# Forming the adaLN modulations of a four-layer network on TensorE alone, 256 columns at a time

## The chip, the cores and the metric

The program runs on one core of a Trainium2 chip, in one launch. The metric is device time in microseconds (us), as the median of three runs; one further execution was profiled, and all rows below are from that one.

## What is computed

Four layers (one mLSTM and differential attention layer, one convolution and mixture-of-experts layer, two hybrid attention layers) work on 256 tokens of width 1024, in fp32. Each is modulated by vectors that depend only on a condition vector c:

```python
def adaln(cond, w, b):
    return jax.nn.silu(cond) @ w + b

# layers 0 and 1: w is 1024 x 6144, six vectors of 1024 each
sh_m, sc_m, gt_m, sh_f, sc_f, gt_f = jnp.split(adaln(c, mod_w, mod_b)[:, None, :], 6, axis=-1)
sh_c, sc_c = jnp.split(adaln(c_ctx, mod_w, mod_b), 6, axis=-1)[:2]      # layer 0 only
# layers 2 and 3: w_ada is 1024 x 3072
shift, scale, gate = jnp.split(c @ w_ada + b_ada, 3, axis=-1)
u = x * (1.0 + scale[:, None, :]) + shift[:, None, :]
```

So each modulation is a product of one row (for the first two vectors of layer 0, of two rows) with a weight matrix: 72 MB of weights in all, read once, with hardly any arithmetic. Everything else of the program (projections, attention, FFN, experts) is products of 256 or 512 tokens with weights.

## The kernel before

All weights come through one stream. `Model.plan` lists them in the order of use; `Stream` loads each as two halves of 512 KB into a ring of eight `raw` buffers of 128 x 1024 (line 164, on SP's DMA queue), and for a projection weight splits each half into an exact high part `hi` (ScalarE, line 98) and a remainder `lo` (VectorE, line 99). The projections then run as three matmuls in a fast fp32 form each (`mm3`, lines 92 to 94: hi x hi, lo x hi, hi x lo). A ring buffer comes free when its last reader is done, and only then is the next load issued.

The modulation weights are items of the same plan, woven between the projection weights (`weave`): 8 items for the first modulation stand alone at the start, about four after each projection weight of layer 0, some 2.75 after each of the four output weights, and the last 24 among the 33 weights of layer 0's FFN. An item is 128 rows of the matrix by 2048 columns, 1 MB, and eight of them make one piece (there are ten pieces; in the last piece of layer 2 and of layer 3 an item has 1024 columns and 0.5 MB). `Ada` treats it in one of two ways.

- The first piece (`vec` is false) multiplies on TensorE: the stationary operand is the condition for these 128 rows, 32 columns wide, and the output lands in one of four groups of 32 PSUM partitions, which are four column groups of TensorE (line 357, `adap<-raw,cond`).
- The other nine pieces (`vec`) scale and add rows elsewhere, in `sum_rows`: the left half of the item on VectorE (lines 337 and 340, tile `adac`), the right half is scaled on ScalarE (lines 338 and 341) and added on GpSimd in two pieces of 512 columns (line 343). After the eighth item TensorE sums the 128 partitions by ones (line 357, `adap<-adac,ones`).

After the eighth item of a piece ScalarE copies the sums out of PSUM (line 364), TensorE transposes them (line 367), and VectorE adds the bias (line 370).

The order of instructions on each engine is made when the program is built, by a list scheduler; each engine then works strictly in that order. So an instruction that waits holds up all that stands behind it on its engine. The PSUM bank that the modulations use (`bg`, one buffer) is shared with the rows that `bcast_row` spreads (line 384).

The names that the rows use: `pf` and `pk` are outputs of layer 0's projections, `rp` rope, `mscan` a running maximum over 256 tokens in 16 dependent steps (line 600), `ds`/`de` and `X`/`E`/`kq`/`pn` the two kinds of attention, `po` the output projection, `ph`/`py` the two products of an FFN, `diag` constants for the convolution that GpSimd prepares (line 1014).

Of the kernel before, what the change touches and what calls it, by code (L numbers as in the profile page):

```python
# [12 lines left out]
F32 = mybir.dt.float32  # L13
# [3 lines left out]
AF = mybir.ActivationFunctionType  # L17
# [14 lines left out]
class Env:  # L32


    def __init__(self, nc, tc, ctx, raw_bufs, split_bufs):
        self.nc, self.tc, self.ctx = nc, tc, ctx
        self.raw_bufs = raw_bufs
        self.cst = ctx.enter_context(tc.tile_pool(name="cst", bufs=1))
        self.small = ctx.enter_context(tc.tile_pool(name="small", bufs=4))
        self.rawp = ctx.enter_context(tc.tile_pool(name="rawp", bufs=raw_bufs))  # L40
        self.splp = ctx.enter_context(tc.tile_pool(name="splp", bufs=split_bufs))
        self.bgp = ctx.enter_context(tc.tile_pool(name="bgp", bufs=2))
        self.bgc = ctx.enter_context(ExitStack())
        self.bgps = self.bgc.enter_context(tc.tile_pool(name="bgps", bufs=1, space=PSUM))
        self.adac = ExitStack()
        self.adasb = self.adac.enter_context(tc.tile_pool(name="adasb", bufs=1, side="right"))
        self.consts()

    def consts(self):
        nc, cst = self.nc, self.cst  # L50
        self.ident = cst.tile([128, 128], F32, name="ident")
        make_identity(nc, self.ident)
        self.identb = cst.tile([128, 128], BF, name="identb")
        nc.vector.tensor_copy(self.identb, self.ident)
        self.ones = cst.tile([128, 128], F32, name="ones")
        nc.vector.memset(self.ones, 1.0)
        zeros = self.adasb.tile([128, 128], F32, name="zeros")
        nc.vector.memset(zeros, 0.0)
        self.mhalf = cst.tile([128, 16], F32, name="mhalf")
        nc.vector.memset(self.mhalf, -0.5)  # L60

        self.tri_le = cst.tile([128, 128], F32, name="tri_le")
        nc.gpsimd.affine_select(self.tri_le, self.ones, [[1, 128]], OP.is_ge, 0.0, base=0, channel_multiplier=-1)
        self.tri_ge = cst.tile([128, 128], F32, name="tri_ge")
        nc.gpsimd.affine_select(self.tri_ge, self.ones, [[-1, 128]], OP.is_ge, 0.0, base=0, channel_multiplier=1)
        self.neg_le = cst.tile([128, 128], BF, name="neg_le")
        nc.gpsimd.affine_select(self.neg_le, zeros, [[1, 128]], OP.is_ge, NEG, base=0, channel_multiplier=-1)
        self.neg_ge = cst.tile([128, 128], BF, name="neg_ge")
        nc.gpsimd.affine_select(self.neg_ge, zeros, [[-1, 128]], OP.is_ge, NEG, base=0, channel_multiplier=1)
# [210 lines left out]
def layout(inputs):  # L280

    a = {k: np.ascontiguousarray(v) for k, v in inputs.items()}
    b = np.zeros((2, 2, 32), np.float32)
    b[:, :, :8] = a.pop("l0_mlstm_gate_b").reshape(2, 2, 8).transpose(1, 0, 2)
    a["gate_b"] = b.reshape(128)
    for g, names in GROUPS.items():
        a[g] = np.ascontiguousarray(np.concatenate([a.pop(k).reshape(-1, 128) for k, _ in names]).T)
    a["lambdas"] = np.concatenate([a.pop("l0_lambda_" + k) for k in ("q1", "q2", "k1", "k2")])
    a["cmp_w1_2"] = np.ascontiguousarray(a["cmp_w1_2"].reshape(2, 2, 16, 128, 64).transpose(0, 1, 3, 2, 4)).reshape(2, 2, 128, 1024)
    a["cmp_w2_2"] = np.concatenate([a["cmp_w2_2"]] * 2, 3)  # L290
    w = a["l0_w_in"]
    a["l0_w_in"], a["l0_w_gate"] = blocks256(w, ORDER), blocked(w, (MG, 32))
    for k in ("l0_ffn_w1", "l0_ffn_w3", "l1_conv_pw1_w", "l1_moe_w1", "l1_moe_w3"):
        a[k] = blocks256(a[k])
    w = a["w_in_2"]
    a["w_in_2"] = np.concatenate([blocked(w, *c) for c in CH], -1)
    a["rope0"] = np.concatenate(rope_axial(), 1)
    a["rope2"] = np.concatenate(rope_plain(64) + rope_plain(32), 1)
    return a
# [12 lines left out]
class Ada:  # L312
# [2 lines left out]

    def __init__(self, e, w, c0, n=2048, vec=False):
        self.e, self.n, self.vec = e, n, vec
        self.items = []  # L320
        for k in range(KB):
            h = [[(w[128 * k:128 * k + 128, c0 + n // 2 * j:c0 + n // 2 * (j + 1)].rearrange("(a p) f -> p a f", p=128),
                   0, n // 2)] for j in range(2)]
            self.items.append(((1, n // 2, h), lambda *t, k=k: self.step(k, t)))

    def bind(self, cond, bias, *out, plus1=None):
        self.cond, self.bias, self.out, self.plus1 = cond, bias, out, plus1

    def sum_rows(self, k, halves):

        e, nc = self.e, self.e.nc
        if k == 0:
            self.acc = e.adasb.tile([128, 2, 1024], F32, tag="adac", name="adac")
        a, (x, y) = self.acc[:, :, :self.n // 2], (h[:, 0, :] for h in halves)
        c = self.cond[:, k, 0:1]
        if k == 0:
            nc.vector.tensor_scalar(a[:, 0], x, c, None, op0=OP.mult)
            nc.scalar.activation(a[:, 1], y, AF.Copy, scale=c)
        else:
            nc.vector.scalar_tensor_tensor(a[:, 0], x, c, a[:, 0], op0=OP.mult, op1=OP.add)  # L340
            nc.scalar.activation(y, y, AF.Copy, scale=c)  # L341
            for i in range(0, self.n // 2, 512):
                nc.gpsimd.tensor_tensor(a[:, 1, i:i + 512], a[:, 1, i:i + 512], y[:, i:i + 512], op=OP.add)  # L343

    def step(self, k, halves):
        e, nc, n = self.e, self.e.nc, self.n
        vec, last = self.vec, k == KB - 1
        if vec:
            self.sum_rows(k, halves)
        if vec and not last:  # L350
            return
        if vec or k == 0:
            self.p = e.bgps.tile([128, 512], F32, tag="bg", name="adap")
        q4 = n // 4
        for j in range(4):
            h = self.acc[:, j // 2] if vec else halves[j // 2][:, 0, :]
            nc.tensor.matmul(self.p[32 * j:32 * j + 32, :q4], e.ones[:, 0:32] if vec else self.cond[:, k, :],
                             h[:, q4 * (j % 2):q4 * (j % 2) + q4],
                             start=(vec or k == 0), stop=last, skip_group_check=True)
        if not last:  # L360
            return
        nb = n // 512
        r = e.bgp.tile([128, 512], F32, tag="adar", name="adar", bufs=1)
        e.ada_read = nc.scalar.copy(r[:, :q4], self.p[:, :q4])
        q = e.bgps.tile([128, 512], F32, tag="bg", name="bg")
        for b in range(nb):
            nc.tensor.transpose(q[:, 128 * b:128 * b + 128], r[:, 128 * b:128 * b + 128], e.ident)
        v = q[:, :128 * nb].rearrange("p (b j r) -> p j b r", b=nb, j=4)
        for i, o in enumerate(self.out):
            nc.vector.tensor_tensor(o.rearrange("p (j b) -> p j b", j=4), v[:, :, :, i],  # L370
                                    self.bias.rearrange("p (j b) -> p j b", j=4), op=OP.add)
            if self.plus1 is not None:
                a, b = self.plus1
                nc.vector.tensor_scalar(o[:, a:b], o[:, a:b], 1.0, None, op0=OP.add)


def bcast_row(e, col, out, n=8):
# [1516 lines left out]
class Model:  # L1894
    def __init__(self, e, I, x, O):
        self.e, self.I, self.x, self.O = e, I, x, O
        self.ada = {}
        if "l0_mod_w" in I:
            for i in range(3):
                self.ada[0, i] = Ada(e, I["l0_mod_w"], 2048 * i, vec=i > 0)  # L1900
        if "l1_mod_w" in I:
            for i in range(3):
                self.ada[1, i] = Ada(e, I["l1_mod_w"], 2048 * i, vec=True)
        if "w_ada_2" in I:
            for l in range(2):
                for i in range(2):
                    self.ada[2 + l, i] = Ada(e, I["w_ada_2"][l], 2048 * i, 2048 - 1024 * i, vec=True)

    def items(self, *keys):
        return [i for k in keys if k in self.ada for i in self.ada[k].items]  # L1910
# [28 lines left out]
    def vecs(self):  # L1939
# [18 lines left out]
        for l in range(2):  # L1958
# [3 lines left out]
            if l == 0:  # L1962
                yield
                with e.tc.issue_after(e.ada_read.ins) if hasattr(e, "ada_read") else ExitStack():
                    load_cols(e, V, I, "vc", q=nc.scalar)
        cond = V["c_2"][:, :, None]
        for l in range(2):
            if (2 + l, 0) in self.ada:
                b = V["b_ada_2"][:, 24 * l:24 * l + 24]
                mods(2 + l, 0, cond, b[:, 0:16], plus1=(8, 16))  # L1970
                mods(2 + l, 1, cond, b[:, 16:24], 8, plus1=(0, 8))
        yield

    def gain(self, mod, g, name):
# [327 lines left out]
```

## Time and profile before

| | us |
|---|---|
| median of three runs | 2024.3 (2023.06 to 2024.95) |
| the profiled execution | 2031.13 |
| its span, first to last instruction | 2029.4 |
| TensorE busy in the span | 1873.0 (92%) |
| VectorE busy | 1582.0 (78%) |
| ScalarE busy | 1189.8 (59%) |
| GpSimd busy | 517.9 (26%) |

The profiled execution is 6.8 us over the median; its span leaves 1.7 us of it outside. Busy shares are averages over stages with different limits, so the stages are to be read apart: from 28 to 392 us layer 0's projections, attention and output projection run, from 392 to 580 us its FFN, then the convolution (to 780), the experts (to about 1550) and the two hybrid layers. The modulations are formed from 0 to 580 us. A matmul that is shown as busy includes the time in which it drains while the next one already runs, so TensorE's busy time overstates its work.

### The profile page before, as it was taken

The numbers are of one execution on the slowest core, as the hardware profiler recorded it, in microseconds if no ns is written. First come the engines' busy times: TensorE is split into PE (matmuls) and PEld (weight loads), VectorE is DVE, ScalarE is ACT, GpSimd is POOL, SyncE is SP. The second block draws the span as 40 slices with busy tenths as digits, with TensorE's granted clock in tenths as the row PEclk, the third lists the DMA queues.
The fourth block names the chain that finished last, engine by engine and source line by source line (L and its number), as shares of the span: only waits on it lengthen the run. The fifth ranks groups of instructions, "written<-read, shape, count | busy, mean of one in ns | idle before, by whom it ended". The sixth has DMA issues, their size and how long they took to land. (4 is left out here: it accounts for less than half of the span.)

```text
span 2029.4 us, 33102 instructions
## 1 busy us (share of the span) xinstructions
PE 1873.0 (92%) x12339; PEld 1657.9 (82%) x12339; DVE 1582.0 (78%) x2239; ACT 1189.8 (59%) x1838; POOL 517.9 (26%) x460
## 2 busy tenths in 40 slices
PE   6789889699997779999999999999997899989997
PEld 3768667699976668999999999999996888878886
DVE  5887996677669758999999999999996674568455
ACT  5455564455545447777777777777776443454333
POOL 2645662533227531000000000000001523333141
PEclk8889987799998889999999999999998988988889
DMA  9845775288753128999999999999993431233120
GB/s 361 285 154 208 244 242 178 80 323 308 250 208 127 50 83 322 366 342 338 346 365 351 333 354 358 342 342 355 355 355 115 135 105 63 89 130 111 65 72 21
DMA packets 132462, 468.41 MB, mean 231 GB/s; under 512 B 14994, under 2 KB 16274, under 8 KB 132292
## 3 DMA queue, kind: packets, MB, share of 16 engines
q1 hardware_dynamic: 131008, 464.38, 64.2%
q8 instruction: 99, 1.62, 0.3%
q10 hardware_dynamic: 1172, 1.65, 0.2%
q14 instruction: 71, 0.58, 0.1%
q0 software_dynamic: 112, 0.17, 0.1%
HBM read 465.10 MB, written 1.05 MB: 230 GB/s over the span
## 5 line engine op out<-in xcount | busy, mean ns | idle before, releaser
L99 DVE TENSOR_TENSOR lo<-raw,hi 128x1024 fp32r<-128x1024 f32 x678 | 858.1, 1280 | 134.9 <-ACT hi L98 112.3
L98 ACT CAST hi<-raw 128x1024 fp32r<-128x1024 f32 x718 | 747.1, 1050 | 300.4 <-PE ph L94 92.8
L93 PE MATMUL ph<-lo,gh 128*128 128x256 f32 x1408 | 397.0, 282 | 3.6 <-DVE lo L99 1.8
L94 PE MATMUL ph<-hi,gl 128*128 128x256 f32 x1408 | 396.7, 282 | 0.0
L92 PE MATMUL ph<-hi,gh 128*128 128x256 f32 x1408 | 394.0, 280 | 0.0
L93 PEld LDWEIGHTS ph<-lo,gh 128*128 128x128 f32 x1408 | 264.6, 188 | 12.6 <-DVE lo L99 6.9
L94 PEld LDWEIGHTS ph<-hi,gl 128*128 128x128 f32 x1408 | 264.8, 188 | 3.4
L92 PEld LDWEIGHTS ph<-hi,gh 128*128 128x128 f32 x1408 | 264.8, 188 | 2.8
L343 POOL TENSOR_TENSOR adac<-adac,raw 128x512 f32<-128x512 f32 x112 | 194.0, 1757 | 180.1 <-ACT raw L341 109.0
L1597 POOL MEMSET kv<- 64x2 f32 x4 | 0.4, 97 | 791.8 <-DVE lo L99 775.1
L99 POOL TENSOR_TENSOR lo<-raw,hi 128x1024 fp32r<-128x1024 f32 (+1 forms) x40 | 97.5, 2446 | 186.9 <-ACT hi L98 178.5
L93 PE MATMUL pe<-lo,hhi 128*128 128x512 f32 x352 | 138.0, 393 | 0.0
L92 PE MATMUL pe<-hi,hhi 128*128 128x512 f32 x352 | 137.2, 397 | 0.5 <-ACT hhi L98 0.5
L94 PE MATMUL pe<-hi,hlo 128*128 128x512 f32 x352 | 125.8, 392 | 0.0
L92 PE MATMUL ht<-hi,Hh 128*128 128x256 f32 (+1 forms) x384 | 117.8, 307 | 0.6 <-ACT u L459 0.6
L93 PE MATMUL ht<-lo,Hh 128*128 128x256 f32 (+1 forms) x384 | 116.0, 302 | 0.0
L94 PE MATMUL ht<-hi,Hl 128*128 128x256 f32 (+1 forms) x384 | 115.8, 302 | 0.0
L92 PE MATMUL ph<-Fh,hi 128*128 128x256 f32 x352 | 101.5, 290 | 11.4 <-DVE h L980 8.8
L93 PE MATMUL ph<-Fl,hi 128*128 128x256 f32 x352 | 101.4, 289 | 0.0
L94 PE MATMUL ph<-Fh,lo 128*128 128x256 f32 x352 | 100.2, 287 | 0.0
L92 PEld LDWEIGHTS ht<-hi,Hh 128*128 128x128 f32 x384 | 79.6, 207 | 2.3 <-ACT u L459 1.4
L1083 POOL TENSOR_TENSOR cyp<-cyp,ctp 128x256 f32<-128x256 f32 x83 | 72.4, 883 | 34.8 <-ACT ctp L1082 31.2
(592 smaller groups left out, 4124.3 us busy)
## 6 DMA issues: line engine op xcount, KB each, us to landing
raw<-in_l_moe_w SPq DMA_DIRECT2D x528, 512.0 KB, 5.3
raw<-in_l_mod_w SPq DMA_DIRECT2D x96, 512.0 KB, 5.4
raw<-in_l_ffn_w SPq DMA_DIRECT2D x66, 512.0 KB, 4.9
raw<-in_w_in SPq DMA_DIRECT2D x60, 512.0 KB, 3.5
raw<-in_w_ada SPq DMA_DIRECT2D x32, 512.0 KB, 5.4
raw<-in_l_w_in SPq DMA_DIRECT2D x28, 512.0 KB, 5.6
raw<-in_l_conv_pw_w SPq DMA_DIRECT2D x24, 512.0 KB, 4.3
raw<-in_w_ada SPq DMA_DIRECT2D x32, 256.0 KB, 3.7
```

What stands on the lines that cost most here:

```text
L92: mm(out, a[0], b[0], start=start, stop=False, **kw)
L93: mm(out, a[0], b[1], start=False, stop=False, **kw)
L94: return mm(out, a[1], b[0], start=False, stop=stop, **kw)
L98: nc.scalar.copy(hi, src)
L99: (lo_eng or nc.vector).tensor_tensor(lo, src, f32(hi), op=OP.subtract)
L343: nc.gpsimd.tensor_tensor(a[:, 1, i:i + 512], a[:, 1, i:i + 512], y[:, i:i + 512], op=OP.add)
L1083: nc.gpsimd.tensor_tensor(yp, yp, t, op=OP.add)
L1597: nc.gpsimd.memset(kv[64:128, :, T - 1:T], 0.0)
```

## The change

All items are now blocks of 256 columns by all 1024 rows (the host lays the three weight matrices out so, as it does for the FFN weights), and every one is multiplied on TensorE. An item takes eight matmuls of 256 columns: for each of the four column groups two, with different 128-row blocks of the weights (`L336` in the rows of the changed kernel). ScalarE copies the 128 x 256 result out (`L339`); TensorE sums the four groups and turns the row into columns with two matmuls whose moving operand `rows4` is one column wide (two for the first piece), `L342`; VectorE adds the bias (and one, where a scale is meant) in one instruction on two columns for each output (`L348`). `sum_rows` is gone. A piece of 2048 columns is still 8 items of 1 MB; one of 1024 columns is 4 items of 1 MB instead of 8 of 0.5 MB, so the items are 72 instead of 80, and 16 instead of 24 of them stand in the FFN.

```diff
+        self.rows4 = cst.tile([128, 3], F32, name="rows4")
+        nc.vector.tensor_reduce(self.rows4, self.ident.rearrange("p (j r) -> p r j", j=4)[:, 0:3, :], axis=AX.X, op=OP.add)
...
-    for k in ("l0_ffn_w1", "l0_ffn_w3", "l1_conv_pw1_w", "l1_moe_w1", "l1_moe_w3"):
+    for k in ("l0_ffn_w1", "l0_ffn_w3", "l1_conv_pw1_w", "l1_moe_w1", "l1_moe_w3", "l0_mod_w", "l1_mod_w", "w_ada_2"):
         a[k] = blocks256(a[k])
...
-    def sum_rows(self, k, halves):
...
-            nc.vector.scalar_tensor_tensor(a[:, 0], x, c, a[:, 0], op0=OP.mult, op1=OP.add)
-            nc.scalar.activation(y, y, AF.Copy, scale=c)
-            for i in range(0, self.n // 2, 512):
-                nc.gpsimd.tensor_tensor(a[:, 1, i:i + 512], a[:, 1, i:i + 512], y[:, i:i + 512], op=OP.add)
...
+    def __init__(self, e, w, c0, n=2048):
+        self.e, self.n = e, n
+        self.items = [(kchunk(w[c0 // 256 + i])[0], lambda *t, i=i: self.step(i, t)) for i in range(n // 256)]
...
+        p = e.bgps.tile([128, 512], F32, tag="bg", name="adap")
+        for f in range(2):
+            for j in range(4):
+                k = 2 * j + f
+                nc.tensor.matmul(p[32 * j:32 * j + 32, :256], self.cond[:, k, :], halves[k // 4][:, k % 4, :],
+                                 start=(f == 0), stop=(f == 1), skip_group_check=True)
+        r = e.bgp.tile([128, 256], F32, tag="adar", name="adar")
+        e.ada_read = nc.scalar.copy(r, p[:, :256])
+        m = len(self.out)
+        for b in range(2):
+            nc.tensor.matmul(p[:, 256 + m * b:256 + m * b + m], r[:, 128 * b:128 * b + 128], e.rows4[:, self.first:self.first + m],
+                             start=True, stop=True, skip_group_check=True)
...
+        for r, o in enumerate(self.out):
+            nc.vector.scalar_tensor_tensor(o[:, cs], v[:, :, r], float(one), self.bias[:, cs], op0=OP.add, op1=OP.add)
```

How the orders move, at three places. The first is TensorE while it makes the first projection (`pf`) and the transposes of the context (`xt`) just after the start. Before, no modulation stands there:

```order
L92 MATMUL pf<-Uh,hi 128x256
L93 MATMUL pf<-Ul,hi 128x256
L94 MATMUL pf<-Uh,lo 128x256
L426 MATMUL xt<-ident,raw 128x128 x16
L92 MATMUL pk<-hi,Uh 128x256
```

In the changed kernel the first woven item (`L336`) opens half-way through these 48 matmuls and stands between them and the transposes (this is the end of the piece; its line numbers are higher by 3 for `mm3`):

```order
L95 MATMUL pf<-Uh,hi 128x256
L96 MATMUL pf<-Ul,hi 128x256
L97 MATMUL pf<-Uh,lo 128x256
L336 MATMUL adap<-raw,cond_114 32x256 x7
L400 MATMUL xt<-ident,raw 128x128 x8
L342 MATMUL adap<-rows_87,adar 128x1 x2
L400 MATMUL xt<-ident,raw 128x128 x8
L336 MATMUL adap<-raw,cond_114 32x256 x8
L95 MATMUL pk<-hi,Uh 128x256
```

So the transposes, and all behind them, now wait for the loads of the first woven item.

The second place is VectorE in the running maximum `mscan` of the gates. Before, sums of the modulation rows (`L340`) and weight splits (`L99`) stand between its steps (`L600`):

```order
L600 TENSOR_TENSOR mscan_635<-mscan_636 32x256
L340 SCALAR_TENSOR_TENSOR adac<-raw,cond_112,adac 128x1024
L600 TENSOR_TENSOR mscan_635<-mscan_636 32x256
L673 TENSOR_TENSOR rp_738<-rp_738,rp_739 128x512
L600 TENSOR_TENSOR mscan_636<-mscan_635 32x256
L99 TENSOR_TENSOR lo<-raw,hi 128x1024
L340 SCALAR_TENSOR_TENSOR adac<-raw,cond_112,adac 128x1024
```

In the changed kernel the same steps (`L574`) follow each other, with one small bias addition between them:

```order
L647 TENSOR_TENSOR rp_819<-rp_819,rp_820 128x512
L574 TENSOR_TENSOR mscan_716<-mscan_715 32x256
L574 TENSOR_TENSOR mscan_715<-mscan_716 32x256
L348 SCALAR_TENSOR_TENSOR mod_1_169<-adap,vb 128x2
L574 TENSOR_TENSOR mscan_715<-mscan_716 32x256
L574 TENSOR_TENSOR mscan_716<-mscan_715 32x256 x2
```

The rows of 1024 columns have left VectorE's order here.

The third place is TensorE in the FFN, where `py` and `ph` follow each other. Before, TensorE meets a modulation there only where a piece ends, as here:

```order
L92 MATMUL ph<-Fh,hi 128x256
L357 MATMUL adap<-adac,ones 32x512
L93 MATMUL ph<-Fl,hi 128x256
L94 MATMUL ph<-Fh,lo 128x256
L92 MATMUL ph<-Fh,hi 128x256
```

In the changed kernel 16 items stand between the matmuls of the FFN, one after every 70 to 120 of them, and the two narrow matmuls (`L342 MATMUL adap<-rows_87,adar 128x1 x2`) of each some 23 rows behind it; only the last one stands behind the last `py`:

```order
L96 MATMUL py<-lo,hhi 128x512
L97 MATMUL py<-hi,hlo 128x512
L336 MATMUL adap<-raw,cond_114 32x256 x8
L95 MATMUL ph<-Fh,hi 128x256
L96 MATMUL ph<-Fl,hi 128x256
L97 MATMUL ph<-Fh,lo 128x256
```

The multiplications have moved into the middle of TensorE's run of FFN matmuls.

## Rows read from the trace of the kernel before

**Rows 1.** Windows: busy us (instructions) of PE, PEld, DVE, ACT, POOL; clock; DMA share; GB/s.

```profile
28.00:392.00 364.00, 305.37 (x1830) 255.25 (x1831) 299.70 (x407) 194.81 (x346) 202.79 (x189) 0.86 0.62 212
392.00:580.00 188.00, 186.51 (x1262) 167.66 (x1260) 121.89 (x136) 97.54 (x129) 47.75 (x31) 0.99 0.75 262
```

**Rows 2.** Waits of TensorE, 28 to 392 us: total us, times, longest.

```profile
PE pf L92 <- DVE rp L671: 10.1, 1, 10.1
PE ph L92 <- DVE h L980: 8.8, 1, 8.8
PE pt L453 <- DVE xs L938: 7.4, 1, 7.4
PE X L745 <- DVE mixd L847: 6.1, 1, 6.1
PE ds L839 <- DVE de L837: 5.8, 3, 4.6
PE ds L831 <- DVE mscan L610: 4.1, 1, 4.1
```

**Rows 3.** Waits of TensorE, 392 to 580 us; the longest of them.

```profile
PE bg L384 <- DVE mod L370: 0.7, 1, 0.7
```

**Rows 4.** Groups, 28 to 392 us: busy us, mean ns, idle before.

```profile
L343 POOL TENSOR_TENSOR adac<-adac,raw 128x512 f32<-128x512 f32 x84 | 147.7, 1788 | 61.5 <-ACT adac L338 23.5 <-ACT raw L341 23.2 <-issue 13.2
...
L340 DVE SCALAR_TENSOR_TENSOR adac<-raw,cond,adac 128x1024 f32<-128x1024 f32 x35 | 62.4, 1782 | 1.1 <-DMA raw<-in_l_mod_w 0.9
L98 ACT CAST hi<-raw 128x1024 fp32r<-128x1024 f32 x45 | 46.9, 1054 | 42.8 <-PE po L94 10.5 <-DMA raw<-in_l_ffn_w 10.3 <-PE pf L93 6.3
...
L340 DVE SCALAR_TENSOR_TENSOR adac<-raw,vc,adac 128x1024 f32<-128x1024 f32 x7 | 13.6, 1937 | 0.0
...
L357 PE MATMUL adap<-adac,ones 128*32 128x512 f32 x44 | 11.6, 605 | 1.2 <-DVE adac L340 1.2
```

**Rows 5.** Groups, 392 to 580 us.

```profile
L357 PE MATMUL adap<-adac,ones 128*32 128x256 f32 (+1 forms) x28 | 6.1, 482 | 0.0
```

**Rows 6.** Timeline of TensorE near 14 us: start us, us; a matmul gives two records.

```profile
13.88 1.06 PE L357 MATMUL adap<-raw,cond 128*32 128x512 f32 x8
```

**Rows 7.** Timeline, 84 to 120 us, the instructions of TensorE around one pair of sums.

```profile
86.36 0.27 PE L94 MATMUL pf<-Uh,lo 128*128 128x256 f32 x1
...
86.57 1.05 PE L357 MATMUL adap<-adac,ones 128*32 128x512 f32 x4
...
87.55 0.57 PE L566 MATMUL gkq<-ident,grow 104*128 104x104 f32 x4
```

**Rows 8.** Timeline, 572 to 580 us: the same sums with 256 columns, their copy, a bias addition.

```profile
576.80 0.63 PE L357 MATMUL adap<-adac,ones 128*32 128x256 f32 x4
...
577.55 0.36 ACT L364 COPY adar<-adap 128x256 f32<-128x256 f32 x1
...
578.93 0.16 DVE L370 TENSOR_TENSOR mod<-bg,vc 128x8 f32<-128x8 f32 x1
```

**Rows 9.** Line 2146, the router: 16 matmuls in fp32 with 8 moving columns; min/median/max ns.

```profile
L2146 PE MATMUL bg<-rw,ru x32: 175/256/361, 736.8 to 740.3; 128*128 128x8 f32 x32
```

**Rows 10.** Timeline of VectorE, 100 to 117 us: steps of the running maximum.

```profile
104.14 0.41 DVE L600 TENSOR_TENSOR mscan<-mscan 32x256 f32<-32x256 f32 x1
...
105.92 1.51 DVE L600 TENSOR_TENSOR mscan<-mscan 32x256 f32<-32x256 f32 x1
```

**Rows 11.** Timeline of VectorE and of GpSimd, 369 us on.

```profile
369.80 16.30 DVE L99 TENSOR_TENSOR lo<-raw,hi 128x1024 fp32r<-128x1024 f32 x3
...
373.07 3.26 POOL L1014 TENSOR_TENSOR diag<-ident,vd 128x128 f32<-128x128 f32 x9
```

**Rows 12.** SP's queue and TensorE's timeline near 40 us; a load's median us to landing.

```profile
38.66 9.95 SPq L164 DMA_DIRECT2D raw<-in_l_mod_w  x8
...
42.45 0.30 PE L426 MATMUL xt<-ident,raw 128*128 128x128 f32 x1 [1.70 <-ACT mghi L98]
...
raw<-in_l_mod_w SPq DMA_DIRECT2D x96, 512.0 KB, 5.4
```

More of the change, by code (lines that the diff above doesn't have):

```diff
@@ L312 @@
 class Ada:
[L318 to L327, printed above, removed]
@@ L329, in sum_rows @@
-    def sum_rows(self, k, halves):
-        e, nc = self.e, self.e.nc
[L332 to L339, printed above, removed]
-            nc.vector.scalar_tensor_tensor(a[:, 0], x, c, a[:, 0], op0=OP.mult, op1=OP.add)
-            nc.scalar.activation(y, y, AF.Copy, scale=c)
-            for i in range(0, self.n // 2, 512):
-                nc.gpsimd.tensor_tensor(a[:, 1, i:i + 512], a[:, 1, i:i + 512], y[:, i:i + 512], op=OP.add)
@@ L345, in step @@
[L345 to L374, printed above, removed]
@@ new lines, in __init__, with bind, step @@
+    def __init__(self, e, w, c0, n=2048):
+        self.e, self.n = e, n
+        self.items = [(kchunk(w[c0 // 256 + i])[0], lambda *t, i=i: self.step(i, t)) for i in range(n // 256)]
+    def bind(self, cond, bias, *out, plus1=None, first=0):
+        self.cond, self.bias, self.out, self.plus1, self.first = cond, bias, out, plus1, first
+    def step(self, i, halves):
+        e, nc = self.e, self.e.nc
+        p = e.bgps.tile([128, 512], F32, tag="bg", name="adap")
[10 more added lines that the diff above has]
+                             start=True, stop=True, skip_group_check=True)
+        v = p[:, 256:256 + 2 * m].rearrange("p (b r) -> p b r", r=m)
+        cs = slice(2 * i, 2 * i + 2)
+        one = self.plus1 is not None and self.plus1[0] <= 2 * i < self.plus1[1]
+        for r, o in enumerate(self.out):
+            nc.vector.scalar_tensor_tensor(o[:, cs], v[:, :, r], float(one), self.bias[:, cs], op0=OP.add, op1=OP.add)
@@ L1899, in __init__ @@
             for i in range(3):
-                self.ada[0, i] = Ada(e, I["l0_mod_w"], 2048 * i, vec=i > 0)
+                self.ada[0, i] = Ada(e, I["l0_mod_w"], 2048 * i)
         if "l1_mod_w" in I:
             for i in range(3):
-                self.ada[1, i] = Ada(e, I["l1_mod_w"], 2048 * i, vec=True)
+                self.ada[1, i] = Ada(e, I["l1_mod_w"], 2048 * i)
         if "w_ada_2" in I:
@@ L1906, in __init__ @@
                 for i in range(2):
-                    self.ada[2 + l, i] = Ada(e, I["w_ada_2"][l], 2048 * i, 2048 - 1024 * i, vec=True)
+                    self.ada[2 + l, i] = Ada(e, I["w_ada_2"][l], 2048 * i, 2048 - 1024 * i)
     def items(self, *keys):
@@ L1965, in vecs @@
                     load_cols(e, V, I, "vc", q=nc.scalar)
-        cond = V["c_2"][:, :, None]
+        if "c_2" in V:
+            nc.vector.tensor_copy(cond[:, :, 2], V["c_2"])
         for l in range(2):
@@ L1969, in vecs @@
                 b = V["b_ada_2"][:, 24 * l:24 * l + 24]
-                mods(2 + l, 0, cond, b[:, 0:16], plus1=(8, 16))
-                mods(2 + l, 1, cond, b[:, 16:24], 8, plus1=(0, 8))
+                mods(2 + l, 0, cond, b[:, 0:16], plus1=(8, 16), first=2)
+                mods(2 + l, 1, cond, b[:, 16:24], 8, plus1=(0, 8), first=2)
         yield
```

## Prediction, before the changed kernel ran

> **What bounds the kernel now.** I first asked for the windows of the two stages in which the modulations are formed [rows 1]. From 28 to 392 us (layer 0 without its FFN) TensorE and VectorE are both busy some 82 to 84% of 364 us, and the granted clock of TensorE averages 0.86, so part of the time it ran at 1.2 and not 2.4 GHz. From 392 to 580 us (the FFN) TensorE is busy 186.5 of 188 us at a clock of 0.99, VectorE 122. Then I read whom TensorE waits for. In the FFN its longest wait is 0.7 us [rows 3]: there TensorE's own matmuls set the end, and nothing that VectorE, ScalarE or GpSimd is relieved of can shorten it. Before it, six waits of four to ten us stand out, all for VectorE [rows 2]. The groups of that stage show what VectorE does meanwhile [rows 4]: 42 additions of modulation rows take 76 us of its 300, and GpSimd is busy 148 us with the other half of the same rows. GpSimd seems to slow VectorE as well: the same step of the running maximum takes 0.41 us in one place and 1.51 us in another, where VectorE and GpSimd both work on modulation rows [rows 10].
>
> So the change relieves one engine in a stage where it is one of two that bind, and loads the other, in that stage and in one that it binds alone. The stages after 580 us hold nothing of the change.
>
> **What an item costs TensorE.** Eight matmuls of 256 columns, two for each column group. The trace has the same kind: four of 512 columns, one in each group, take 1.06 us together [rows 6], no more than two take (1.05) [rows 7], so the groups run at once. With 256 columns it is 0.63 [rows 8]; 256 columns thus stream in 1.05 - 0.63 = 0.42 us, and an item in 0.85. What it displaces is longer, since the array changes between four groups and the whole: from the last full matmul before such a pair, at 86.36, to the next full instruction, at 87.55, is 1.19 us, of which the last matmul itself has about 0.12 (the following pair of rows would start that much later) [rows 7]. That is 1.07 for the streaming of 512 columns with both changes.
>
> On such changes the Trainium skill has a rule that speaks against the kernel: TensorEngine Tiling, Key Properties, says that changing the tiling mode drains TensorE. By [rows 7] a change costs about 0.1 us on either side, which is less than the drain that a group shows beyond its streaming (0.63 - 0.42 = 0.21 us); if each change waited for a full drain of that length, as the rule would have it, the 64 items would cost 64 x 2 x 0.11 = 14 us more than I count.
>
> The two narrow matmuls behind an item have 128 x 128 fp32 weights and one moving column. The nearest row is the router's, with such weights and 8 columns: 32 records from 736.8 to 740.3 us, 0.11 us each [rows 9]; a matmul is two records, so the two cost 0.45 us. The Trainium skill would make them cheaper: TensorEngine Tiling, Instruction Overhead, gives each matmul about 60 cycles and a single column the time of 60. At 2.4 GHz that is an estimate of 0.1 us for the four records, or 22 us less over 64 items; the row has the same weights, so I go by it.
>
> An item is therefore 1.07 + 0.45 = 1.52 us of TensorE at full clock. Below, without the changes and with half the records, 0.85 + 0.22 = 1.07; above, with both changes drained, 1.07 + 0.22 + 0.45 = 1.74. Over the 64 new items that is 97 us, between 68 and 111. The eight items of the first piece were on TensorE before; they pass while the first 8 MB load, and I count them at nothing (what shows of them, the last one's narrow matmuls, replaces four transposes).
>
> The other engines gain. ScalarE copies 128 x 256 in 0.36 us and VectorE adds a bias in 0.16 us an item [rows 8]; the 48 items before the FFN give VectorE 8 us for the 76 it loses.
>
> **The FFN.** 16 items at 1.52 are 24 us. The last stands behind the last matmul of the FFN, beside the residual: 23 us remain. Removed are 28 records of sums, 6 us [rows 5], and 12 transposes (four for each of three pieces), which at the 0.14 us of the transposes of `gkq`, four in 0.57 [rows 7], are 2. With TensorE the bound [rows 1, 3] the difference goes straight into the time: **+15 us**. No cover is left there that could hide it.
>
> **Before the FFN.** 48 items at 1.52 are 73 us. Removed are 44 records of sums, which as eleven groups of four at 1.07 make 12 us [rows 4, 7], and 24 transposes, 3 us. So TensorE gets 58 us more work in a stage of 364 us in which it is shown busy 305 [rows 1]. What is given back:
> - the waits for VectorE: rope 10.1, `mixd` 6.1, `de` 5.8 and `mscan` 4.1 us, 26 in all [rows 2]. They stand behind work that leaves VectorE. I take them all. The other two I leave: `h` (8.8) comes after three splits that took 16.3 us while GpSimd made the convolution's `diag` [rows 11], which stays, and `xs` (7.4) is the end of the residual's chain.
> - the clock. At 0.86 over 364 us, of which TensorE is busy 84%, at most 0.14 x 364 x 0.84 = 43 us are lost to the lower level. Items in the gaps make TensorE steadier; I take a third, 14. Nothing excludes 0 or all.
> - places where TensorE has nothing else: the order puts five items ahead of the output projection and two beside the residual, seven items, of which I take six as free, 9 us.
> Against it stand:
> - the start. The first woven item now stands ahead of the context's transposes. Its loads are issued from 38.66 us on [rows 12]; with 5.4 us to land, the first half is there at about 44, while the transposes began at 42.45. With the item's own 1 to 2 us and the second half behind it, 4 us. VectorE's free time may win it back by the next chunk.
> - new waits. Each item adds a step TensorE to ScalarE, back to TensorE, to VectorE, and only then is the one PSUM bank free. The scheduler has put some 23 matmuls between, near 2.8 us, for a copy of 0.36. I take 4 us in all; nothing bounds this from the trace but ScalarE's queue (below).
>
> Sum: 58 - 26 - 14 - 9 + 4 + 4 = **+17 us**.
>
> **Sum.** 17 + 15 = 32 us. On the profiled execution, 2031.1 us, that gives 2063; it is 7 us over the median of the runs, so on the median it gives **2056 us**, 1.6% slower. The price of an item moves it by -29 or +14.
>
> **The rivals.**
> - *VectorE alone bound the stage before the FFN.* Then its relief pays for TensorE's new work there, and only the FFN's 15 us show: 2039 us. For it speak [rows 2]; against it TensorE's 305 us, which with 58 more fill 363 of 364 unless the clock rises.
> - *It comes out faster.* The one mechanism is the clock: if the items keep TensorE at 2.4 GHz from 28 to 392 us, all 43 us come back and not 14, and the items cost the lower bound, 1.07. Then the 48 items cost 22 us less (0.45 each) and the work is 58 - 22 = 36; less 26, 43 and 9, plus 4 for the start, that makes -38. In the FFN 15 items at 1.07 less the 8 removed are +8. Together -30: 2024 - 30 = 1994 us. It decides in favour of the change once stage one ends 15 us earlier. Against it: part of the lower clock lies at the very start and around the residual, where TensorE waits for chains that no item fills.
> - *The coupling.* TensorE works in order, and so does ScalarE. If the narrow matmuls of an item find ScalarE in one cast (1.05 us, [rows 4]) that the scheduler did not foresee, TensorE stands for it: 64 x 1.05 = 67 us, of which perhaps half lie in the pass of the 23 matmuls ahead. 2056 + 36 = 2092 us. For it speaks that ScalarE is kept waiting itself before its casts, 43 us [rows 4]; against it the distance.
>
> **How the numbers follow.** My sum and its near surroundings (2043 to 2075) get 0.50, the first rival 0.17, the faster one 0.13, the coupling 0.20. The range leaves out the faster rival and the upper part of the coupling: 2024 to 2090. A measurement of this kernel can tell some 0.2% (4 us) from no change: faster 0.14, the same 0.06, slower 0.80.
>
> **What would show it.** In the changed profile: the FFN, from its first to its last `py`, longer by 15 us with no new waits; an item's eight matmuls with their narrow ones, 1.5 us apart from the rest; the waits for rope, `mixd`, `de` and `mscan` gone; VectorE some 70 us less busy before the FFN and GpSimd almost idle; the first `ph` about 17 us later. I am wrong if the FFN does not grow (then TensorE was not its bound, or the groups run faster than the rows say), or if the clock before the FFN comes near 1.0 and the first `ph` earlier, or if waits of TensorE for the copies (`adar`) or for loads add up to more than 10 us.

## The result, and the profile after

The changed kernel takes 2099.95 us (median of four runs, 2097.31 to 2100.62) where the kernel before, run beside it, takes 2024.62: a ratio of 1.0364 with the 95% interval [1.0343, 1.0386], or 75 us. The forecast was slower by 32 us, 2056 us, with a range to 2090. The profiled execution of the changed kernel has a span of 2095.6 us, 66 more than that of before (whose profiled execution was 6.8 us over its median, while this one is 2.6 under).

The program is cut by what TensorE starts: the first projection matmul (`pf`), the first `ph` and the first and last `py` of the FFN. The windows of the kernel before between these points are (columns as in [rows 1]):

```profile
31.10:365.80 334.70, 287.29 (x1718) 238.82 (x1718) 274.85 (x391) 182.16 (x329) 176.90 (x134) 0.87 0.64 219
405.20:576.90 171.70, 171.70 (x1164) 154.79 (x1164) 114.56 (x124) 89.74 (x116) 46.84 (x29) 1.00 0.80 279
```

and those of the changed kernel, with the stretch before the first `pf` ahead of them:

```profile
0.00:50.80 50.80, 28.45 (x176) 15.79 (x176) 14.78 (x45) 15.77 (x28) 4.71 (x18) 1.00 0.81 288
50.80:423.80 373.00, 343.77 (x2614) 271.05 (x2614) 162.23 (x382) 143.18 (x321) 30.29 (x54) 0.91 0.54 192
456.20:644.70 188.50, 188.50 (x1414) 165.41 (x1416) 85.60 (x107) 74.53 (x104) 0.57 (x1) 1.00 0.70 233
```

| stretch | before | after | difference | forecast |
|---|---|---|---|---|
| start to first `pf` | 31.1 | 50.8 | +19.7 | 0 (the 4 us for the start were laid to the transposes behind it) |
| first `pf` to first `ph` | 334.7 | 373.0 | +38.3 | +17 |
| first `ph` to first `py` | 39.4 | 32.4 | -7.0 | 0 |
| first to last `py` | 171.7 | 188.5 | +16.8 | +15 |

So the FFN came as forecast, and the two earlier stretches did not. VectorE did lose its rows before the FFN (275 to 162 us busy) and GpSimd almost everything (177 to 30). TensorE took 56 us more busy time there, and its granted clock rose only from 0.87 to 0.91.

**The start.** The timeline of TensorE in the changed kernel from 19 us on (start, us, line, tiles; in brackets the idle time before and what ended it) shows the first piece's items (`L336`) and their narrow matmuls (`L342`):

```profile
20.62 1.94 PE L336 MATMUL adap<-raw,cond 128*32 128x256 f32 x16 [0.43 <-PE adap L342]
23.12 1.01 PE L342 MATMUL adap<-rows,adar 128*128 128x2 f32 x4 [0.57 <-ACT adar L339]
24.57 1.93 PE L336 MATMUL adap<-raw,cond 128*32 128x256 f32 x16 [0.43 <-PE adap L342]
...
32.46 1.93 PE L336 MATMUL adap<-raw,cond 128*32 128x256 f32 x16 [0.43 <-PE adap L342]
39.12 1.01 PE L342 MATMUL adap<-rows,adar 128*128 128x2 f32 x4 [4.73 <-ACT adar L339]
40.57 1.93 PE L336 MATMUL adap<-raw,cond 128*32 128x256 f32 x16 [0.43 <-PE adap L342]
```

An item is a closed ring: its matmuls, the copy by ScalarE, the narrow matmuls, the bias addition by VectorE, and only then the one PSUM bank is free for the next item. At 3.95 us an item (20.62 to 24.57) the eight take 31.6 us, more than the 28 us within which their 8 MB were loaded and multiplied in the kernel before. One copy is waited for 4.73 us. It stands behind the casts of the first projection weights in ScalarE's order, and ScalarE itself stood 5.54 us for the load of such a weight:

```profile
36.49 1.04 ACT L101 CAST hi<-raw 128x1024 fp32r<-128x1024 f32 x1 [5.54 <-DMA raw<-in_l_w_in]
...
38.70 0.37 ACT L339 COPY adar<-adap 128x256 f32<-128x256 f32 x1
```

And the 16 records take 1.93 us where the same ones take 1.07 after 60 us: nearly twice as long, so TensorE ran at its lower level (1.2 GHz), though the windows print 1.00 for this stretch. In the kernel before as many columns for each group took 1.06 us at 13.88 us already [rows 6]. The lower level is probably a part of the loss: at the upper one a round took 2.6 us (356.23 to 358.82, below), and eight of them would be 21 us, less than the 28. That is an estimate; no run separates the ring from the level here. The layout of the blocks is not the cause: late_tail, below, loads the same blocks at 401 to 424 GB/s from 4 to 34 us, and the kernel before loaded at 389 to 422.

**Before the FFN.** TensorE's longest waits from 50.8 to 424 us (line waiting, what it waited for, total us, times, longest) answer to [rows 2]:

```profile
PE adap L336 <- DVE mod L348: 10.2, 12, 2.7
PE adap L342 <- ACT adar L339: 6.1, 8, 2.4
PE adap L336 <- ACT gtb L359: 3.0, 2, 2.3
PE xt L400 <- ACT cvx L629: 1.9, 2, 1.4
...
PE ds L813 <- DVE de L811: 1.3, 2, 0.9
```

The waits for rope, `mixd` and `mscan` are gone, as forecast; the wait for `de` is down to 1.3 us. Three waits that the items themselves bring are at the top instead, 19 us. Some 12 of these 19 us stand where the items follow each other with little or no other work (358 to 372 and 405 to 422 us), in the places I had called free. This is the timeline ahead of the output projection:

```profile
356.23 1.07 PE L336 MATMUL adap<-raw,cond 128*32 128x256 f32 x16
...
358.82 1.07 PE L336 MATMUL adap<-raw,cond 128*32 128x256 f32 x16 [0.35 <-DVE mod L348]
...
364.22 1.93 PE L336 MATMUL adap<-raw,cond 128*32 128x256 f32 x16 [0.68 <-ACT gtb L359]
366.73 1.01 PE L342 MATMUL adap<-rows,adar 128*128 128x1 f32 x4 [0.57 <-ACT adar L339]
368.06 1.93 PE L336 MATMUL adap<-raw,cond 128*32 128x256 f32 x16 [0.32 <-DVE mod L348]
```

From 364 us an item is 3.84 us, at the lower level and with nothing between.

**The price of an item** was right. In the FFN it stands among full matmuls:

```profile
514.03 0.27 PE L97 MATMUL ph<-Fh,lo 128*128 128x256 f32 x1
514.24 1.07 PE L336 MATMUL adap<-raw,cond 128*32 128x256 f32 x16
515.24 0.50 PE L95 MATMUL py<-hi,hhi 128*128 128x512 f32 x1
```

From the last `ph` at 514.03, less its 0.12, to the first `py` at 515.24 are 1.09 us; the forecast had 1.07, and [rows 8] gave it.

### The profile page after: what moved, and what is told of

It reads as the page before. It is cut to its first block, busy times and chain, and to the rows that moved or that the text cites. A ratio compares the mean times of both kernels' runs of the same rounds, so it can differ in the third digit from the quotient of the medians.

```text
span 2095.6 us, 35432 instructions
## 1 busy us (share of the span) xinstructions
PE 1949.0 (93%) x13607; PEld 1707.6 (81%) x13607; DVE 1448.0 (69%) x2234; ACT 1138.8 (54%) x1828; POOL 321.8 (15%) x348
## 5 line engine op out<-in xcount | busy, mean ns | idle before, releaser
L102 DVE TENSOR_TENSOR lo<-raw,hi 128x1024 fp32r<-128x1024 f32 x678 | 840.7, 1254 | 171.9 <-ACT hi L101 145.7
L336 PE MATMUL adap<-raw,cond 128*32 128x256 f32 x1152 | 97.1, 454 | 25.6 <-DVE mod L348 10.2
L339 ACT COPY adar<-adap 128x256 f32<-128x256 f32 x72 | 26.9, 374 | 115.6 <-PE adap L336 115.3
L336 PEld LDWEIGHTS adap<-raw,cond 128*32 128x32 f32 x1152 | 34.6, 122 | 60.0 <-issue 20.8
```

The source lines that it names most:

```text
L102: (lo_eng or nc.vector).tensor_tensor(lo, src, f32(hi), op=OP.subtract)
L336: nc.tensor.matmul(p[32 * j:32 * j + 32, :256], self.cond[:, k, :], halves[k // 4][:, k % 4, :], start=(f == 0), stop=(f == 1), skip_group ...
L339: e.ada_read = nc.scalar.copy(r, p[:, :256])
```

## The experiments

All are compared with the kernel before on their own chip by the ratio, since its median differed from chip to chip (2025.7 to 2030.6 us). The stretches are from one profiled execution each.

My theory after the result: the item's tail (copy, narrow matmuls, bias addition in one bank) is what was mispriced, at the start (20 us) and before the FFN (some 25), while TensorE's own work was priced rightly. The rivals were that the start is made up later, that the narrow matmuls are dearer than their records show, and that the matmuls themselves are the loss.

**first_rows**: the first piece as in the kernel before (`AdaRows` is the old `Ada`, which reads the old layout).

```diff
+ROWS = ((0, 0),)
...
-                self.ada[0, i] = Ada(e, I["l0_mod_w"], 2048 * i)
+                self.ada[0, i] = (AdaRows(e, I["l0_mod_w_r"], 2048 * i, vec=(0, i) != (0, 0)) if (0, i) in ROWS
+                                  else Ada(e, I["l0_mod_w"], 2048 * i))
```

> The changed kernel with its first piece formed as before: eight items of 128 rows by 2048 columns that accumulate in PSUM, one copy and four transposes at the end. My theory: in the changed kernel each of the first eight items is a closed chain (8 matmuls 1.93 us, copy, narrow matmuls 1.01, bias addition, 3.95 us an item in one PSUM bank), which delays the first projection matmul from 31.1 to 50.8 us; with the old way it starts at 31 to 33 us again, and the whole gains 17 to 21 us: 2080 us. Rival: the late start is made up later, since loads and VectorE set the pace of the first projections; then the first projection moves but the whole gains under 6 us: 2095 us.

Measured: ratio 1.0268 [1.0227, 1.0309], median 2081.0 us. The first `pf` is at 31.96 us and the last `py` ends 19 us earlier than in the changed kernel:

```profile
29.05 0.66 PE L372 MATMUL bg<-ident,adar 128*128 128x128 f32 x4 [0.69 <-ACT adar L369]
31.96 0.80 PE L95 MATMUL pf<-Uh,hi 128*128 128x256 f32 x2 [2.26 <-ACT Uh L483]
```

Nothing of it is made up later: the stage behind it takes 371.8 us as against 373.0.

```profile
32.00:403.80 371.80, 342.03 (x2614) 270.83 (x2615) 168.76 (x388) 147.01 (x327) 31.34 (x55) 0.91 0.56 200
```

**ffn_rows**: the three pieces of the FFN as before (the same edit with `ROWS = ((2, 1), (3, 0), (3, 1))`).

> The changed kernel with the three pieces of the FFN summed over rows on VectorE, ScalarE and GpSimd as before. My theory: TensorE alone sets the end there, so the FFN from its first to its last py takes 172 us again and not 188.5, and the whole gains 15 to 18 us: 2083 us. Rival: with VectorE's casts and sums and GpSimd back, TensorE waits for them in an FFN that now starts in another state of the loads, and less than 8 us come back.

Measured: ratio 1.0310 [1.0273, 1.0347], median 2089.7 us. The FFN takes 171.5 us again, to the tenth what it took before:

```profile
457.00:628.50 171.50, 169.21 (x1158) 154.26 (x1158) 113.64 (x117) 86.31 (x112) 43.87 (x26) 1.00 0.78 268
```

17 us go with the items there, though the profiled span falls by 13.5 and the ratio by 0.54%, that is 11 us where 15 to 18 were expected: the stretch between the FFN's end and the first expert matmul (`pe`) was 4.9 us longer (201.4 and 196.5). It holds nothing of the change and varied by as much in other runs (196.2 to 202.0); I did not find why.

**two_halves**: the bank used as two halves in turn (`self.t` is one tile of 512 columns).

```diff
+        c = 256 * (self.n % 2)
+        return self.t[:, c:c + shape[1]]
...
-        p = e.bgps.tile([128, 512], F32, tag="bg", name="adap")
+        p = e.bgps.tile([128, 256], F32, tag="bg", name="adap")
...
-            nc.tensor.matmul(p[:, 256 + m * b:256 + m * b + m], r[:, 128 * b:128 * b + 128], e.rows4[:, self.first:self.first + m],
+            nc.tensor.matmul(p[:, m * b:m * b + m], r[:, 128 * b:128 * b + 128], e.rows4[:, self.first:self.first + m],
```

> The changed kernel with the one PSUM bank used as two halves of 256 columns in turn, and the two narrow matmuls writing over the sums that were copied; the spreading of rows goes in four steps of 256 columns and not two of 512. My theory: TensorE's waits for the bias addition and for the bank (10 and 3 us from 51 to 424 us, and about 0.4 us an item in the first piece) go, 12 to 18 us in all: 2085 us; the waits for the copy stay. Rival: what waits is the copy behind ScalarE's queue, and the bank's release only comes last; then under 4 us come back: 2097 us.

Measured: ratio 1.0360 [1.0327, 1.0394], no gain. But the edit did not do what it was for. TensorE still waits for the bias addition of the item just before, which reads the other half (waits of TensorE, 20 to 425 us):

```profile
PE bg L355 <- ACT adar L352: 13.3, 14, 3.0
PE bg L349 <- DVE mod L361: 13.0, 12, 4.4
```

Both halves are parts of one tile in the program, which probably orders them as one; that is not shown. So the run says nothing on either theory.

**no_tail**: no tail for 55 of the 64 items behind the first piece (`chain` is true for the first piece alone). The modulations of these columns stay at the bias.

```diff
+        if (self.first or not self.chain) and i < len(self.items) - 1:
+            return
         r = e.bgp.tile([128, 256], F32, tag="adar", name="adar")
```

> The changed kernel without the tail of an item (copy, two narrow matmuls, bias addition) for 55 of the 64 items behind the first piece; the modulations of these columns are left at the bias, so the output is not the reference's. My theory: the tail costs TensorE 0.5 us of streaming and, before the FFN, as much again in waits: 13 items of the FFN give back 6 to 8 us, 42 items before it 21 us of streaming and 15 to 20 us of waits; in all 42 to 50 us: 2054 us. Rival A: the tail costs its streaming alone: 27 us, 2073 us. Rival B: a single moving column is nearly free: the FFN gives back under 3 us.

Measured: ratio 1.0090 [1.0059, 1.0120], 2049.1 us. The FFN gives back 5.3 us (183.1; 6 to 8 were expected), that is 0.41 for each of 13 tails, and the stage before it 51, more than the 36 to 41 expected:

```profile
52.70:374.80 322.10, 306.84 (x2446) 238.63 (x2446) 156.96 (x345) 126.88 (x275) 28.01 (x51) 0.98 0.62 224
```

With the matmuls of all 48 items and hardly a tail this stage is 12.6 us *shorter* than in the kernel before (334.7), and its clock is 0.98 (0.97 with its first 7 us, in which the matmuls' lengths tell the lower level and the record does not). So relieving VectorE and GpSimd was worth more than TensorE's new matmuls cost; the tails took it away, 1.2 us each where their streaming is 0.44. What a tail takes from ScalarE and VectorE went with it in this run.

**late_tail**: one tail for a piece (`self.acc` is a row buffer for the piece).

```diff
-        r = e.bgp.tile([128, 256], F32, tag="adar", name="adar")
-        e.ada_read = nc.scalar.copy(r, p[:, :256])
...
+        e.ada_read = nc.scalar.copy(self.acc[:, 256 * i:256 * i + 256], p[:, :256])
+        if i < len(self.items) - 1:
+            return
+        m, nb = len(self.out), 2 * len(self.items)
+        p = e.bgps.tile([128, 512], F32, tag="bg", name="bg")
+        for b in range(nb):
+            nc.tensor.matmul(p[:, m * b:m * b + m], self.acc[:, 128 * b:128 * b + 128], e.rows4[:, self.first:self.first + m],
...
```

> The changed kernel with one tail for a piece and not for each item: an item's sums are copied to a row buffer in SBUF and its PSUM bank is free after that; behind the last item 16 narrow matmuls follow each other, and one bias addition. The same matmuls in all. My theory: of the 51 us that the stage from the first pf to the first ph lost without tails, only the 20 us of streaming stay, the rest was the chain copy, narrow matmuls, bias addition and the lower clock behind its waits: the stage takes 340 to 350 us and not 373, the first piece shrinks by 8 to 12 us, the FFN stays at 187 to 189: in all 35 to 45 us, 2060 us. Rival: the narrow matmuls themselves cost that much (128 x 128 weights for one column, one change of the array for each): then the stage stays above 360 us and the whole above 2082 us.

Measured: ratio 1.0237 [1.0207, 1.0266], 2075.1 us, a gain of 25 us where 35 to 45 were expected. The first `pf` is at 39.6 us (11 us earlier), the FFN at 189.1, and the stage takes 358.7, between the theory and its rival:

```profile
39.60:398.30 358.70, 337.11 (x2586) 265.75 (x2586) 159.43 (x339) 140.85 (x317) 27.79 (x51) 0.93 0.57 201
```

The price of the narrow matmuls is not the reason. A stretch of 16 of them is 3.49 us, 0.11 for each of the 32 records, just as the router's were [rows 9]. But see what follows one (timeline, then windows, where the clock stands ahead of the DMA share):

```profile
134.10 3.63 PE L346 MATMUL bg<-rows,adac 128*128 128x1 f32 x32
137.59 0.36 PE L95 MATMUL pk<-hi,Uh 128*128 128x256 f32 x1
```

```profile
134.00:138.00 4.00, 4.00 (x38) 4.00 (x37) 0.55 (x3) 0.46 (x2) 0.00 (x0) 1.00 0.40 162
138.00:142.00 4.00, 4.00 (x23) 4.00 (x22) 0.14 (x1) 0.00 (x0) 0.00 (x0) 0.57 0.00 0
243.00:255.00 12.00, 12.00 (x63) 8.72 (x62) 5.00 (x13) 3.82 (x13) 0.11 (x2) 0.57 0.02 8
333.00:344.00 11.00, 11.00 (x66) 10.04 (x65) 3.26 (x11) 2.03 (x4) 1.07 (x2) 0.69 0.13 50
```

TensorE is shown busy without a gap in the stretch and behind it, and yet its clock is at the lower level in most of the window from 138 us on. The last two windows show the same in or behind the stretches at 242.5 and 332.7 us; behind those at 184.4 and 286.8 us the clock stayed up. Nor do they hold most of it: of the some 50 us that this stage spends at the lower level, about 20 are in these three windows and 10 between 150 and 164 us (clock 0.63), where no such stretch is; the rest is at its two ends and near 57 and 358 us.

**late_mix, late_mix2, late_mix4**: late_tail with the first piece and the FFN's pieces as before, and with one and three further pieces as before (the edit of first_rows with longer lists).

> late_tail with the first piece and the three pieces of the FFN formed as in the kernel before. If the three costs add, first projection at 32 us, stage of 345 us, FFN of 172 us: 2030 to 2036 us, that is within 0.6% of the kernel before. Rival: the costs overlap (what the start gains is waited for later), then 2045 us or more. Under 2020 us only if TensorE's clock stays up in the stage.

> late_mix with one more piece (the scale and shift of layer 2) formed as before, so that five of six pieces ahead of the FFN are on TensorE. By the account of TensorE's work 12 us less in the stage; if VectorE's 14 us of sums are hidden there: 2020 to 2024 us. Rival: the sums of this piece stand where VectorE holds up the end of attention and the residual, and nothing is gained on late_mix.

> late_mix with three more pieces formed as before, so that half of the six pieces ahead of the FFN are on TensorE and half on VectorE, ScalarE and GpSimd. If both engines bind that stage and the work is shared between them: stage of 322 us, 2012 us. Rival: the waits for VectorE (rope, running maximum) come back with its sums and TensorE's work stays: stage of 340 us, 2030 us.

Measured: 1.0167 [1.0139, 1.0196], 1.0127 [1.0101, 1.0153] and 1.0034 [1.0015, 1.0054], that is 2065.1, 2056.7 and 2033.3 us: all three slower than expected. The gains do not add: late_mix starts its first `pf` 8 us before late_tail, yet its first `ph` comes only 2 us before, and the time from there to the first `py` is 43 us and not 33. Its stage is the longer one, at a clock of 0.90:

```profile
31.40:396.00 364.60, 345.35 (x2587) 272.91 (x2587) 164.95 (x346) 145.21 (x324) 30.74 (x52) 0.90 0.57 204
```

So the rival held for the first; why the clock is lower than in late_tail (0.93) stays open. In late_mix2 the stage is 363.3 us, hardly shorter, as its rival had it. late_mix4 comes out near its rival's numbers too (stage 336.0, 2033 us), but not by its mechanism: no wait for rope or the running maximum is among TensorE's.

**lag_tail**: the two narrow matmuls of an item issued with the next item, out of the row buffer (`tail` holds them and the bias addition).

```diff
+        if i == 0:
...
+        else:
+            self.tail(p, i - 1)
+        e.ada_read = nc.scalar.copy(self.acc[:, 256 * i:256 * i + 256], p[:, :256])
+        if i == len(self.items) - 1:
+            self.tail(e.bgps.tile([128, 512], F32, tag="bg", name="bg"), i)
```

> The changed kernel with the two narrow matmuls of an item issued one item later, out of a row buffer: they wait for no copy that is under way, and do not stand in stretches of 16 as in late_tail. If the stretches of narrow matmuls are what lowers TensorE's clock in late_tail (51 us at the lower level from the first pf to the first ph), this falls under 30 us and the whole is 2062 to 2068 us. Rival: the clock follows the waits, and the bank is again held until the bias addition: 2075 to 2090 us.

Measured: ratio 1.0174 [1.0142, 1.0207], 2060.7 us, a little under the theory's 2062 to 2068. The work is that of late_tail and of the changed kernel, every narrow matmul included:

```profile
42.50:383.00 340.50, 324.46 (x2614) 257.37 (x2614) 163.12 (x380) 140.76 (x317) 27.70 (x51) 0.98 0.60 213
```

TensorE's clock is 0.98, the stage 340.5 us: 18 less than late_tail, 32.5 less than the changed kernel. From the clock, the time at the lower level is (1 - 0.98) x 2 x 340.5 = 14 us here, 50 in late_tail (0.93 over 358.7) and 67 in the changed kernel (0.91 over 373). TensorE idles 16.0 us here and 21.6 in late_tail, so waits make at most 6 of the 18. In the changed kernel it idles 29.2: of the 32.5 us, 13 are waits, and 19 are busy time that shrank with as many matmuls (2614 records in both), which I lay to the clock.

**acc1, acc3, acc5**: the kernel before with one, three and five more pieces formed as its first piece is, on TensorE, accumulated over their eight items in PSUM, one copy and four transposes at the end. The edit is one flag (here acc5):

```diff
-                self.ada[0, i] = Ada(e, I["l0_mod_w"], 2048 * i, vec=i > 0)
+                self.ada[0, i] = Ada(e, I["l0_mod_w"], 2048 * i, vec=False)
-                self.ada[1, i] = Ada(e, I["l1_mod_w"], 2048 * i, vec=True)
+                self.ada[1, i] = Ada(e, I["l1_mod_w"], 2048 * i, vec=False)
```

> The kernel before, with one more piece (gate and shift of layer 0) formed as its first piece is: eight items on TensorE that accumulate in PSUM, one copy and four transposes for the piece. TensorE gets 8 items at about 1.07 us less one group of sums, 7 to 8 us; VectorE loses 14 us and GpSimd 24 in the stretch of the running maximum. If the waits for rope and the running maximum (14 us) go with them: stage from the first pf to the first ph 325 to 330 us and 2017 to 2021 us. Rival: TensorE's work decides: 342 us, 2031 us.

> The kernel before with three more pieces accumulated on TensorE, as its first is (24 items, no tail in an item). By my account 26 us of work on TensorE less 4 us of sums, and 20 to 30 us of waits and lower clock come back: stage of 325 to 335 us, 2015 to 2024 us. Rival (the work alone decides, as it did when the tails were gathered): 350 us and 2040 us.

> The kernel before with five more pieces accumulated on TensorE, all that stand ahead of the FFN but one (40 items). The kernel without tails took 322 us for 48 items: if the tails are what the changed kernel lost there, 325 to 335 us here and 2015 to 2025 us. Rival: the matmuls of the items themselves (43 us) are as dear as the waits they replace: 345 to 355 us, 2035 to 2045 us.

Measured: 1.0002 [0.9981, 1.0022], 0.9956 [0.9938, 0.9975] and 0.9966 [0.9948, 0.9984]. acc3 (2019.3 us) and acc5 (2020.0) are faster than the kernel before by some 0.4% and 0.3%, little, but their intervals leave out 1. The windows of acc3 and acc5 from the first `pf` to the first `ph`:

```profile
31.60:355.30 323.70, 293.81 (x1887) 230.64 (x1887) 215.38 (x368) 155.70 (x305) 98.73 (x92) 0.93 0.65 226
```

```profile
31.00:345.90 314.90, 295.31 (x1999) 226.74 (x1999) 181.26 (x352) 140.00 (x289) 53.25 (x64) 0.97 0.64 233
```

With 40 of the 48 items on TensorE in acc5 and no tail in them its stage is 20 us shorter than before. The matmuls were not the loss. Only part of this shows in the times: the profiled span of acc5 is 13 us shorter, its median 6, for the execution of the kernel before that was profiled lay over its median and that of acc5 2 us under. acc1's stage is 324.3 us, about as expected, but its FFN took 175.6 (171.7 before) and the stretch ahead of that 43.6 (39.4), so its time is that of before.

## Why the prediction was wrong

**The step that failed first** is the sentence on the first piece: "The eight items of the first piece were on TensorE before; they pass while the first 8 MB load, and I count them at nothing." They were on TensorE before, but without a tail. The ring of each item through ScalarE, TensorE and VectorE in one bank makes 3.95 us at TensorE's lower level, eight of them last longer than the loads, and 19.7 us are lost. first_rows shows the place: undone alone, it gives 19 us. That the tails are in it is shown by late_tail, which starts 11 us earlier with one tail for the piece. The 4 us that I set for the start were laid to something else, the context's transposes; those waited only 1.9 us in the changed kernel (`cvx`, a ScalarE copy, not a load).

**The second** is the stage before the FFN, +17 with the 4 us of the start, 13 without them, and 38.3 measured. By its terms:

- *Work, +58.* Right: 48 items at 1.07 and their narrow matmuls at 0.44. TensorE's busy time, less what the lower level adds to it (37 us before, 34 after, see the clock), rises from 250 to 310 us, by 60.
- *Waits and free places, -26, -9 and +4 for new waits, together -31.* TensorE's time that is not busy falls from 47.4 to 29.2 us, 18 only. The old waits went as forecast. The step that failed is "I take 4 us in all": the items' own waits are 19 us (10.2 + 6.1 + 3.0), and the "six as free" are among them, since items that follow each other without other work run at the pace of their ring. My coupling rival named a cast ahead of the copy as the cause; the waits for the copy are the smaller part (6.1), and seven of these eight are under 0.7 us, little more than the copy itself; the bank's release by the bias addition is the larger part (10.2).
- *The clock, -14.* By the same formula as in the prediction it gave back 3: 0.13 x 334.7 x 0.86 = 37 us lost before; after, 0.09 x 373 x 0.92 = 31 and 3 more for the first 6 us of the stage, where the record shows no lower level but the same matmuls start 0.21 us apart and from 57 us on 0.12. That nearly all of it can come back with the items on TensorE is shown by no_tail and lag_tail (0.97 and 0.98); what stood against it were the tails.

60 - 18 - 3 is 39, the 38.3 measured up to rounding, as it must be, since busy and idle time make up the stage; the split into work and clock rests on the formula. Against the forecast of 13, the waits miss by 13, the clock by 11 and the work by 2.

**What was right.** The FFN: +15 forecast, 16.8 measured, and ffn_rows takes all of it away; no wait of TensorE is shown there. By that the narrow matmul's price from the router's row holds (0.11 us a record), and not the Trainium skill's figure for a single column (TensorEngine Tiling, Instruction Overhead), from which I had worked out an estimate of 0.1 us for the four records; late_tail's 3.49 us for 32 records make 0.44. The Trainium skill's rule that a change of the tiling mode drains TensorE (TensorEngine Tiling, Key Properties) would have made an item dearer; the 1.09 us at 514 us show about 0.1 on either side again. Not foreseen were the 7 us that the stretch from the first `ph` to the first `py` gave back; the wait for `h`, 8.8 us before, is 5.1 after, and one of 2.6 for `Fh` is gone.

The side was right, and the size off by more than a factor of two. The nearest rival was the coupling (2092 us; half of its 67 us is 34 and not 36, so 2090), for a largely other reason: that its number is near is luck. The faster rival had the right mechanism (relief and a higher clock outweigh the work before the FFN), but for items without a ring in each: acc5's stage is 20 us shorter than that of before, lag_tail's, with the ring only loosened, 6 longer.

## What to carry to other kernels

When work moves to an engine, price the ring that each item closes (its copy, its way back, the release of its buffer) beside its streaming, and look for places where items follow each other with nothing between: there the ring, not the streaming, sets the pace. A step that "was there before" has to be read again for what is new in it. An accumulation over items that ends in one tail was worth more here than items that each end in their own: ahead of the FFN, 40 accumulated items made the stage 20 us shorter than before (acc5), and the 48 of the changed kernel made it 38 longer.

## What the runs showed of the hardware

TensorE can be shown busy all the time and still fall to the lower level: in late_tail it did behind 16 narrow matmuls, busy for the whole of 134 to 142 us. With the same matmuls in twos, in lag_tail, the clock stayed at 1.00 from 60 to 330 us:

```profile
60.00:120.00 60.00, 60.00 (x428) 50.34 (x427) 28.34 (x67) 18.31 (x39) 5.08 (x14) 1.00 0.27 96
120.00:160.00 40.00, 40.00 (x361) 30.87 (x359) 18.41 (x45) 16.97 (x44) 0.72 (x5) 1.00 0.63 219
160.00:330.00 170.00, 167.89 (x1439) 133.84 (x1439) 73.11 (x183) 65.07 (x155) 9.88 (x19) 1.00 0.64 228
```

That the stretch is the cause was expected before lag_tail ran and fits it, but lag_tail also moved other matmuls, two of late_tail's stretches were not followed by the lower level, and more than half of late_tail's time at that level lies elsewhere: not shown. At the start a printed clock of 1.00 is no proof of the upper level: in the changed kernel the item's 16 records took 1.93 us until 48 us, and 1.07 from 60 us on, as they take 1.93 from 364 us on, where the printed clock is 0.72 (356 to 374 us). The same shows in a full matmul of the first projection:

```profile
54.72 0.41 PE L95 MATMUL pf<-Uh,hi 128*128 128x256 f32 x1
...
57.06 0.28 PE L95 MATMUL pf<-Uh,hi 128*128 128x256 f32 x1
```
